# A gate projection ahead of the transposes, a norm in pieces, two merge blocks at the entry, and retention transposes on TensorE

## The chip, the cores and the metric

The kernel runs on one core of a Trainium2 chip. The metric is the device time of one execution in microseconds (us), taken over several runs; their median is compared.

## What is computed

Two transformer blocks follow each other on x of 1024 tokens by 1024 features, in float32. The first (neighbourhood attention beside a gated delta rule) is not touched by the change. The second reads, cut to what matters here:

```
h = rms_norm(x, norm_gain)
proj = einsum('bsd,dc->bsc', h, w_in)            # 1024 -> 10240 columns
(sb_q, sb_k, sb_v, sb_g, r_q, r_k, r_v, r_g, m_sb, m_ret) = split(proj)
qa, ka = rms_norm(heads(sb_q), q_gain), rms_norm(heads(sb_k), k_gain)      # 8 heads of 128
out_a = merge(stick_breaking_attention(qa, ka, heads(sb_v))) * silu(sb_g)
qb, kb = rotary(heads(r_q)), rotary(heads(r_k)) * RET_KEY_DIM ** -0.5      # 4 heads of 256
ret = chunkwise_retention(qb, kb, heads(r_v))
#   out   = (q * q_decay) @ state + (q k^T * intra_decay) @ v
#   state = state * chunk_decay + (k * k_decay)^T @ v
out_b = merge(rms_norm(ret, ret_out_gain)) * silu(r_g)
merged = sigmoid(m_sb + b0) * (out_a @ w_branch_sb) + sigmoid(m_ret + b1) * (out_b @ w_branch_ret)
x = x + merged @ w_out
```

## The kernel before, in words

Every large product runs in three passes: both operands are split into a high and a low part, and TensorE (PE) sums high·high, high·low and low·high in one PSUM bank. A product over 1024 features therefore takes 24 matmuls for each bank. The activations `h2T` (high `h2h`, low `h2l`) stand in SBUF with the features on the partitions. Weights are loaded in units of 128 rows and split either by ScalarE (ACT) and VectorE (DVE), lines 67 and 68, or by GpSimd (POOL), lines 70 and 71.

PSUM has three banks "a" for projections, two "z", and one each of "t", "o" and "p". Code is written in stages, and a scheduler then fixes the order of the instructions on each engine ahead of the run; at run time each engine works through its list in that order and waits where an input is late.

The stages after the first block, with their places in the profiled span:

- **Output projection and norm** (740 to 830 us). The tokens are worked on as two sets: set 0 is the two middle quarters, set 1 the outer two. Blocks of 128 output features are computed in set 0 and then, in the order 4 to 7 and 0 to 3, in set 1 (`out_blocks`, L859). Each is added to x on DVE (`residual`, L866), which frees its PSUM bank. `normalize` makes the RMS norm of one set: the squares' sum over features goes through PE (L897, L903), a reciprocal root goes through POOL (L125, L126), and then eight times DVE scales a block (L909), ACT takes its high part, and POOL or DVE its low part (L911).
- **Stick-breaking heads** (830 to 1340 us), eight in a row. A head projects q, k and v for eight groups of 128 tokens (`dense_tok`, L102), takes their norm (ACT L980, POOL L125 and L126, DVE L986), which frees the bank, and after every fourth group turns q and k by PE transposes (L993). Head 0 works by token set, so that it can begin with set 0 before set 1 is normed, and its gate projection stands in the same loop (L1003). The attention itself uses PE transposes into the banks "t" and "p" (L1050).
- **Merge projection** (`merge_logits`, L112 and L956): its quarter 0 follows the heads, the other three follow retention. Each quarter is four column blocks of 48 matmuls, 128 partitions by 512.
- **Retention** (1400 to 1940 us), four heads; `ret_proj` projects and rotates q and k (L1095 to L1100: DVE products, POOL sums, tile `ro`) and projects v (L102, L1109). `ret_chain` works in two groups of four chunks for each head. In each group k is turned so that tokens stand on partitions (`kf`), scaled and split into `kd` (ACT L1154, DVE L1155), and multiplied with v into the state (L1184, L1190, L1195). The chunk outputs `ot` (L1178) are turned back into `ob`, scaled (ACT L1201) and gated (POOL L1202). Both turns go through `dve_transpose`, 16 DVE instructions on 32x32 blocks (L132). `kf` and `ob` share one buffer.
- **Branches and output** (to 2279 us).

Of the kernel before, what the change touches and what calls it, by code (L numbers as in the profile page):

```python
# [11 lines left out]
F32 = mybir.dt.float32  # L12
# [7 lines left out]
P = 128  # L20
# [16 lines left out]
def tile_kernel(ctx: ExitStack, tc: tile.TileContext, I: dict, out: bass.AP, dbg=None, stop=None):  # L37
# [161 lines left out]
    sm = ctx.enter_context(tc.tile_pool(name="sm", bufs=1))  # L199
# [675 lines left out]
    sc_.__exit__(None, None, None)  # L875
    naB.__exit__(None, None, None)
# [6 lines left out]
    with tc.tile_pool(name="dd", bufs=1) as dd:  # L883
        XB = 10

        def square_sum(qa, xo, first):
            if first:
                nc.scalar.activation(out=qa, in_=xo, func=AF.Square)
                return
            sq = dd.tile([P, 512], F32, tag="sq", name="sq", bufs=2)  # L890
            nc.scalar.activation(out=sq, in_=xo, func=AF.Square)
            nc.vector.tensor_tensor(out=qa, in0=qa, in1=sq, op=ALU.add)

        def normalize(s, xs, qa):
            ps = bank("z")
            for j in range(4):
                nc.tensor.matmul(ps[:, 2 * j:2 * j + 2], lhsT=qa[:, j * P:(j + 1) * P], rhs=ones2, start=True, stop=True)  # L897
            rt_ = dd.tile([P, 4], F32, tag="rt", name="rt_", bufs=2)
            nc.vector.tensor_copy(out=rt_, in_=ps[:, 0:8:2])
            rsqrt_small(rt_, rt_, 1.0 / T, EPS, 4)  # L900
            pr = bank("t")
            for j in range(4):
                nc.tensor.matmul(pr[:, j * P:(j + 1) * P], lhsT=rt_[:, j:j + 1].to_broadcast([P, P]), rhs=ident,  # L903
                                 start=True, stop=True)
            rs = dd.tile([P, 512], F32, tag="rs", name="rs")
            nc.scalar.copy(out=rs, in_=pr)
            for k in range(NK):
                hi, lo = [token_set(h[:, k, :], s) for h in h2T]
                nc.vector.scalar_tensor_tensor(out=xs[k], in0=xs[k], scalar=gain2[:, k:k + 1], in1=rs, op0=ALU.mult, op1=ALU.mult)  # L909
                nc.scalar.copy(out=hi, in_=set2(xs[k]))  # L910
                (nc.gpsimd, nc.vector)[k % 2].tensor_tensor(out=lo, in0=set2(xs[k]), in1=f32(hi), op=ALU.subtract)  # L911

        xs = {}
        qa = dd.tile([P, 512], F32, tag="qa", name="qa")
        for b in range(4):
            xs[b] = dd.tile([P, 512], F32, tag="xo", name="x0", bufs=XB)
            nc.sync.dma_start(out=set2(xs[b]), in_=token_set(d_x1[b], 0))
            square_sum(qa, xs[b], b == 0)
        us = load_units(I["w_out"], 512, 512, fast=True)
        for b in range(4, 8):  # L920
            xs[b] = residual(dd, "xo", XB, out_blocks(us, 0, (b,))[0], 0, b)
            square_sum(qa, xs[b], False)
        normalize(0, xs, qa)
        xs = {}
        qa = dd.tile([P, 512], F32, tag="qa", name="qa")
        for half in (1, 0):
            if half == 0:
                us = load_units(I["w_out"], 0, 512, fast=True)
            for b in range(4 * half, 4 * half + 4):
                xs[b] = residual(dd, "xo", XB, out_blocks(us, 1, (b,))[0], 1, b)  # L930
                square_sum(qa, xs[b], b == 4)
        normalize(1, xs, qa)
# [14 lines left out]
    mp = ctx.enter_context(tc.tile_pool(name="mp", bufs=1))  # L947
    bm = mp.tile([P, 16], F32, name="bm")
    nc.sync.dma_start(out=bm, in_=I["b_merge_2"])

    def merge_logits(q):
# [11 lines left out]
    with tc.tile_pool(name="sb", bufs=1) as sb, tc.tile_pool(name="sr", bufs=1, side="right") as sr:  # L963
# [4 lines left out]
        for h in range(8):  # L968
# [4 lines left out]
            for n_, (m, acc) in enumerate(dense_tok(h2T, us, 0, 384, order=order)):  # L973
                j = n_ % 4
                if j == 0:
                    sq4 = sr.tile([P, 4, 256], F32, tag="sq", name="sq", bufs=2)
                sq = sq4[:, j, :]
                ss = sr.tile([P, 2], F32, tag="ss", name="ss", bufs=2)
                for a in range(2):
                    nc.scalar.activation(out=sq[:, a * P:(a + 1) * P], in_=acc[:, a * P:(a + 1) * P], func=AF.Square,  # L980
                                         accum_out=ss[:, a:a + 1])
                rsqrt_small(ss, ss, 1.0 / P, EPS, 2)
                nc.scalar.copy(out=v[0][:, m, :], in_=acc[:, 256:384])
                nc.vector.tensor_tensor(out=v[1][:, m, :], in0=acc[:, 256:384], in1=f32(v[0][:, m, :]), op=ALU.subtract)
                for a in range(2):
                    nc.vector.scalar_tensor_tensor(out=sq[:, a * P:(a + 1) * P], in0=acc[:, a * P:(a + 1) * P],  # L986
                                                   scalar=ss[:, a:a + 1], in1=gqk[:, a, :], op0=ALU.mult, op1=ALU.mult)
                if j == 3:
                    sl = slice((m - 3) * P, (m + 1) * P)
                    for a in range(2):  # L990
                        qa = bank("a")
                        for jj in range(4):
                            nc.tensor.transpose(qa[:, jj * P:(jj + 1) * P], sq4[:, jj, a * P:(a + 1) * P], ident)  # L993
                        hi, lo = [t_[:, sl] if h else token_set(t_, n_ // 4) for t_ in qk[a]]
                        if h == 0:
                            qa = set2(qa)
                        nc.scalar.copy(out=hi, in_=qa)
                        nc.vector.tensor_tensor(out=lo, in0=qa, in1=f32(hi), op=ALU.subtract)
                if j == 3 and h == 0:
                    acc = bank("a")  # L1000
                    for k in range(NK):
                        for i, (x, y) in enumerate(((0, 0), (1, 0), (0, 1))):
                            nc.tensor.matmul(acc, lhsT=us[k][:, y, 384:512], rhs=token_set(h2T[x][:, k, :], n_ // 4),  # L1003
                                             start=(k == 0 and i == 0), stop=(k == NK - 1 and i == 2))
                    gv = mp.tile([P, 512], F32, tag="lg", name="gv", bufs=2)
                    nc.scalar.copy(out=gv, in_=acc)
                    nc.sync.dma_start(out=token_set(d_ga[h], n_ // 4), in_=set2(gv))
# [57 lines left out]

    merge_logits(0)
# [4 lines left out]
    with tc.tile_pool(name="rt", bufs=1) as rt:  # L1071
# [61 lines left out]
        def ret_chain(h, tiles):  # L1133
            qTs, kTs, vs = tiles
            state = None
            for g in range(2):
# [14 lines left out]
                kf = rt.tile([P, 4, 256], F32, tag="ob", name="kf")  # L1151
                dve_transpose(kf.rearrange("p n (b c) -> p b n c", b=2), kT.rearrange("p b (n c) -> p b n c", n=4))
                kf, kh, kl = [t_.rearrange("p a b -> p (a b)") for t_ in [kf] + kd]
                nc.scalar.activation(out=kh, in_=kf, func=AF.Copy, scale=rdv[:, h, 0:1])  # L1154
                nc.vector.scalar_tensor_tensor(out=kl, in0=kf, scalar=rdv[:, h, 0:1], in1=f32(kh),  # L1155
                                               op0=ALU.mult, op1=ALU.subtract)
# [51 lines left out]
    for q in range(1, 4):  # L1208
        merge_logits(q)
# [130 lines left out]
```

## Time and profile before

| | us |
|---|---|
| median of 3 runs | 2288.43 |
| lowest and highest | 2281.9, 2291.71 |
| the profiled execution's own time | 2281.08 |
| its span | 2279.4 |

The page of the profile gives each engine's busy time as a share of the span. Its matmul durations overlap each other, since PE is pipelined: the time from the start of one to the start of the next is what a matmul costs, and the chain that ended last gives that in its piece for a row of matmuls.

### The profile page before, as it was taken

To read this page: it belongs to the slowest core of one execution; us is meant where nothing else is said; L and a number is where in the kernel's file an instruction comes from. 1 tells how busy PE (TensorE), PEld (TensorE's weight loads), DVE (VectorE), ACT (ScalarE), POOL (GpSimd) and SP (SyncE) were. 2 spreads that over 40 slices of the span, in tenths; PEclk is the share of its full clock that TensorE was granted. 3 is DMA by queue.
4 is the path that set the end of the run, shared out by engine and by line. 5 is a ranking of instruction groups with operands and counts; after the bars stand their busy time and mean duration, and the time that the engine had idled before them with its cause. 6 is when DMAs were issued, how large, how long until landed. Compare 5 with 4: busy or idle time off the path is not lost.

```text
span 2279.4 us, 33389 instructions
## 1 busy us (share of the span) xinstructions
PE 2171.1 (95%) x12197; PEld 1872.3 (82%) x12197; DVE 1222.5 (54%) x2228; ACT 763.6 (33%) x1904; POOL 1107.4 (49%) x1435
## 2 busy tenths in 40 slices
PE   7999888899999989999999999999989999999999
PEld 7777777687888878899999988888878788788887
DVE  4688789943457474556566541417474744321321
ACT  5344433445455233334344331112222222321200
POOL 6668787762003253333344442537575744444531
PEclk9999999999999999999999999999999999999999
DMA  4256830045386441111111113111333232654432
GB/s 131 85 155 163 206 109 26 36 118 165 103 301 228 148 131 47 54 33 36 56 56 52 56 61 103 37 65 56 130 112 129 84 107 93 222 171 153 148 107 102
DMA packets 238788, 249.23 MB, mean 109 GB/s; under 512 B 40032, under 2 KB 173856, under 8 KB 238368
## 3 DMA queue, kind: packets, MB, share of 16 engines
q1 hardware_dynamic: 238624, 247.10, 34.2%
q8 instruction: 96, 1.57, 0.3%
q14 instruction: 68, 0.56, 0.1%
HBM read 171.51 MB, written 75.53 MB: 108 GB/s over the span
## 4 chain that ended last, share of the span: by engine, by line
PE 54%; POOL 5%; issue 3%; DMA 2%; DVE 2%; ACT 1%; SPq 0%; POOLq 0%; ACTq 0%
PE acc L112 29%; PE acc L102 13%; PE acc L859 3%; PE po L1055 2%; PE pz L1023 2%; POOL wu L71 1%; POOL wu L70 1%; PE pt L1050 1%; PE pt L1171 1%; DMA d_oag<-oa 1%; DMA oa<-d_oa 1%; PE acc L1003 1%; POOL ob L1202 1%; PE pp L1050 0%; PE acc L120 0%
## 5 line engine op out<-in xcount | busy, mean ns | idle before, releaser
L112 PE MATMUL acc<-h2h,wu 128*128 128x512 f32 x1504 | 460.1, 396 | 0.7 <-POOL wu L71 0.4
L102 PE MATMUL acc<-wu,h2h 128*128 128x384 f32 (+1 forms) x1536 | 370.0, 324 | 6.8 <-DVE v L1109 4.0
L71 POOL TENSOR_TENSOR wu<-raw,wu 128x512 fp32r<-128x512 f32 (+3 forms) x268 | 364.1, 1367 | 7.0
L70 POOL TENSOR_SCALAR wu<-raw 128x512 fp32r<-128x512 f32 (+3 forms) x268 | 206.4, 773 | 330.1 <-PE acc L112 249.1
L112 PEld LDWEIGHTS acc<-h2h,wu 128*128 128x128 f32 x1504 | 282.1, 188 | 65.4 <-ACT lg L956 1.2
L102 PEld LDWEIGHTS acc<-wu,h2h 128*128 128x128 f32 x1536 | 268.0, 191 | 12.7 <-DVE v L1109 4.9
L112 PE MATMUL acc<-h2l,wu 128*128 128x512 f32 x752 | 278.3, 395 | 0.0
L102 PE MATMUL acc<-wu,h2l 128*128 128x384 f32 (+1 forms) x768 | 246.0, 321 | 0.0
L102 PE MATMUL acc<-wu,h1hi 128*128 128x384 f32 (+2 forms) x768 | 192.0, 333 | 12.6 <-DVE kS L518 6.7
L112 PE MATMUL acc<-h1hi,wu 128*128 128x512 f32 x512 | 165.8, 412 | 6.8 <-ACT pad L315 3.3
L125 POOL TENSOR_SCALAR ss<-ss 128x2 f32<-128x2 f32 (+2 forms) x136 | 37.1, 273 | 277.6 <-ACT sq L980 218.8
L112 PEld LDWEIGHTS acc<-h2l,wu 128*128 128x128 f32 x752 | 141.2, 188 | 31.1
L102 PEld LDWEIGHTS acc<-wu,h1hi 128*128 128x128 f32 x768 | 137.1, 195 | 17.0 <-issue 8.0
L102 PEld LDWEIGHTS acc<-wu,h2l 128*128 128x128 f32 x768 | 146.1, 190 | 1.9
L102 PE MATMUL acc<-wu,h1lo 128*128 128x384 f32 (+2 forms) x384 | 126.7, 333 | 0.0
L112 PEld LDWEIGHTS acc<-h1hi,wu 128*128 128x128 f32 x512 | 99.2, 195 | 31.7 <-ACT pad L315 4.4
L126 POOL TENSOR_TENSOR ss<-ss,mhalf 128x2 f32<-128x2 f32 (+2 forms) x136 | 119.2, 877 | 8.6
L112 PE MATMUL acc<-h1lo,wu 128*128 128x512 f32 x256 | 96.9, 407 | 0.0
L980 ACT ACTIVATE sq<-acc 128x128 f32<-128x128 f32 x128 | 35.6, 289 | 128.5 <-PE acc L102 124.4
L320 DVE SCALAR_TENSOR_TENSOR cv<-pad,c_conv_w,cv 128x1024 f32<-128x1024 f32 x48 | 76.6, 1596 | 1.1
L112 PE MATMUL acc<-oah,wu 128*128 128x512 f32 x256 | 76.9, 396 | 0.0
L1055 PE MATMUL po<-wT,v 128*128 128x512 f32 (+3 forms) x288 | 74.7, 351 | 1.7 <-DVE wT L1053 1.3
(546 smaller groups left out, 4471.5 us busy)
## 6 DMA issues: line engine op xcount, KB each, us to landing
raw<-in_w_in_dram SPq DMA_DIRECT2D x192, 256.0 KB, 2.9
d_pk<-sct SPq DMA_DIRECT2D x24, 512.0 KB, 4.3
raw<-in_w_out_dram SPq DMA_DIRECT2D x40, 256.0 KB, 2.6
wsa<-d_pk SPq DMA_DIRECT2D x16, 512.0 KB, 5.5
wsb<-d_pk SPq DMA_DIRECT2D x16, 512.0 KB, 7.6
d_sg<-lg SPq DMA_DIRECT2D x32, 256.0 KB, 2.5
sg<-d_sg SPq DMA_DIRECT2D x32, 256.0 KB, 3.6
raw<-in_w_in_dram SPq DMA_DIRECT2D x32, 192.0 KB, 2.7
```

The costliest lines, as they stand in the source:

```text
L70: nc.gpsimd.tensor_scalar(out=u[:, 0, :], in0=raw, scalar1=1.0, scalar2=0.0, op0=ALU.mult, op1=ALU.add)
L71: nc.gpsimd.tensor_tensor(out=u[:, 1, :], in0=raw, in1=f32(u[:, 0, :]), op=ALU.subtract)
L102: nc.tensor.matmul(acc[:, :n], lhsT=hT[a][:, k, m * P:(m + 1) * P], rhs=us[k][:, b, c0:c0 + n], start=(k == 0 and i == 0), stop=(k == NK - ...
L112: nc.tensor.matmul(accs[half], lhsT=us[k][:, b, c0:c0 + P], rhs=hT[a][:, k, half * 512:(half + 1) * 512], start=(k == 0 and i == 0), stop= ...
L125: nc.gpsimd.tensor_scalar(out=dst, in0=src, scalar1=mul, scalar2=eps, op0=ALU.mult, op1=ALU.add)
L126: nc.gpsimd.tensor_tensor(out=dst, in0=dst, in1=mhalf[:, :eshape], op=ALU.pow)
L320: nc.vector.scalar_tensor_tensor(out=cv, in0=pad[:, i:i + T], scalar=conv_w[:, blk, i:i + 1], in1=cv, op0=ALU.mult, op1=ALU.add)
L859: nc.tensor.matmul(acc, lhsT=us[k][:, y, (b % 4) * P:(b % 4 + 1) * P], rhs=token_set(mT[x][:, k, 0:T], s), start=(k == 0 and i == 0), stop ...
L980: nc.scalar.activation(out=sq[:, a * P:(a + 1) * P], in_=acc[:, a * P:(a + 1) * P], func=AF.Square, accum_out=ss[:, a:a + 1])
L1003: nc.tensor.matmul(acc, lhsT=us[k][:, y, 384:512], rhs=token_set(h2T[x][:, k, :], n_ // 4), start=(k == 0 and i == 0), stop=(k == NK - 1 a ...
L1023: nc.tensor.matmul(pz[:, :w], lhsT=qk[0][a][:, i * P:(i + 1) * P], rhs=qk[1][b][:, c0:c0 + w], start=(x == 0), stop=(x == 2))
L1055: nc.tensor.matmul(po[:, i0 * P:512], lhsT=v[a][:, c0 // P + kb, :], rhs=wT[b][:, :n], start=(diag and kb == 0 and x == 0), stop=(diag == ...
```

## The change

It has four parts.

1. `normalize` becomes a generator, and pieces of it are asked for after each block of the output projection (set 0) and after each token group of head 0 (set 1). Some pools open and close at other places, and the number of `xo` buffers goes from 10 to 9.
2. In head 0 the gate projection is written ahead of the transposes of q and k.
3. Two of the sixteen merge blocks (12 and 13) are computed at the entry, by token set, from weights of their own in a pool "fp": 16 more split instructions on POOL and 8 DMAs of 128 KB. Three of their four banks are asked for in head 0 and the last at head 1. The last quarter of the merge projection after retention keeps two blocks.
4. In retention both turns go to PE, as 16 transposes of 128x128 for each group, into bank "p". ACT and DVE read them from PSUM. `dve_transpose` is gone, and `kf` too.

```diff
-    def dve_transpose(dst, src):
-
-        for a in range(4):
-            for b in range(4):
-                nc.vector.transpose(out=dst[32 * b:32 * b + 32, :, :, 32 * a:32 * a + 32],
-                                    in_=src[32 * a:32 * a + 32, :, :, 32 * b:32 * b + 32])
...
+        nc.scalar.copy(out=rs, in_=pr)
+        yield 1
+        for k in range(NK):
...
+            (nc.gpsimd, nc.vector)[k % 2].tensor_tensor(out=lo, in0=set2(xs[k]), in1=f32(hi), op=ALU.subtract)
+            yield 1
...
+    norm = normalize(0, xs, qa)
...
+            square_sum(qa, xs[b], b == 4)
+            take(norm, 3 if b == 4 else 1)
+    drain(norm)
+    norm = normalize(1, xs, qa)
...
+    def early_logits():
+
+        us = load_units(I["w_in_2"], 8192 + 12 * P, 256, pool=fp, tag="fu")
+        for s in range(2):
+            for b in range(2):
+                acc = bank("a")
+                for k in range(NK):
+                    for i, (x, y) in enumerate(((0, 0), (1, 0), (0, 1))):
+                        nc.tensor.matmul(acc, lhsT=us[k][:, y, b * P:(b + 1) * P], rhs=token_set(h2T[x][:, k, :], s),
+                                         start=(k == 0 and i == 0), stop=(k == NK - 1 and i == 2))
...
+                yield 1
+
+    early = early_logits()
...
+                if h == 0:
+                    take(norm, 3)
...
+                if j == 3 and h == 0:
+                    acc = bank("a")
...
+                    nc.sync.dma_start(out=token_set(d_ga[h], n_ // 4), in_=set2(gv))
+                    if n_ == 3:
+                        drain(norm)
+                        dd_.__exit__(None, None, None)
+                        sb = sbs.enter_context(tc.tile_pool(name="sb", bufs=1))
+                    take(early, 1 + (n_ == 3))
                 if j == 3:
                     sl = slice((m - 3) * P, (m + 1) * P)
                     for a in range(2):
...
-                if j == 3 and h == 0:
-                    acc = bank("a")
...
+            if h == 1:
+                drain(early)
...
-                kf = rt.tile([P, 4, 256], F32, tag="ob", name="kf")
-                dve_transpose(kf.rearrange("p n (b c) -> p b n c", b=2), kT.rearrange("p b (n c) -> p b n c", n=4))
...
+                for x in range(2):
+                    pk = bank("p")
+                    for j in range(2):
+                        for b in range(2):
+                            n = 2 * x + j
+                            nc.tensor.transpose(pk[:, j * 256 + b * P:j * 256 + (b + 1) * P], kT[:, b, n * P:(n + 1) * P], ident)
...
+                    nc.scalar.activation(out=kh, in_=pk, func=AF.Copy, scale=rdv[:, h, 0:1])
...
-                dve_transpose(ob, ot.rearrange("p n (b c) -> p b n c", b=2))
...
+                    pt = bank("p")
+                    for j in range(4):
+                        nc.tensor.transpose(pt[:, j * P:(j + 1) * P], ot[:, j, b * P:(b + 1) * P], ident)
...
-        merge_logits(q)
+        merge_logits(q, range(2, 4) if q == 3 else range(4))
```

`take(g, n)` runs n steps of a generator, and `drain(g)` the rest. The order of the compiled instructions changes at three places.

**The set 0 norm on DVE**, behind the second block of set 1 (about 790 us in the span). Before, the sum of x and the second block, and one sum of squares, stand ahead of the eight scalings L909:

```order
L899 COPY rt__7971<-pz 128x4
L866 TENSOR_TENSOR xo<-acc,xo 128x512
L892 TENSOR_TENSOR qa<-qa,sq 128x512
L909 SCALAR_TENSOR_TENSOR x_7780<-x_7780,c_norm_gain_7774,rs 128x512
...
L909 SCALAR_TENSOR_TENSOR xo<-xo,c_norm_gain_7774,rs 128x512 x4
...
L911 TENSOR_TENSOR h2l<-x_7793,h2h 128x512
L866 TENSOR_TENSOR xo<-acc,xo 128x512
L911 TENSOR_TENSOR h2l<-xo,h2h 128x512
```

In the changed kernel (L866 is now L860, L909 is L911, L911 is L913):

```order
L900 COPY rt__8011<-pz 128x4
L911 SCALAR_TENSOR_TENSOR x_7789<-x_7789,c_norm_gain_7775,rs 128x512
...
L911 SCALAR_TENSOR_TENSOR xo<-xo,c_norm_gain_7775,rs 128x512 x4
...
L913 TENSOR_TENSOR h2l<-x_7802,h2h 128x512
L860 TENSOR_TENSOR xo<-acc,xo 128x512
L913 TENSOR_TENSOR h2l<-xo,h2h 128x512
L68 TENSOR_TENSOR wu<-raw,wu 128x512
L860 TENSOR_TENSOR xo<-acc,xo 128x512
```

The sum of the second block, which frees its bank, has moved behind all eight scalings and two low parts.

**Head 0 on PE**, where its first four token groups end. Before, the eight transposes of q and k stand directly behind the last projection, and the gate projection behind them:

```order
L102 MATMUL acc<-wu,h2h 128x384 x2
L102 MATMUL acc<-wu,h2l 128x384
L993 MATMUL acc<-ident,sq 128x128 x8
L1003 MATMUL acc<-h2h,wu 128x512
L1003 MATMUL acc<-h2l,wu 128x512
```

In the changed kernel 24 matmuls of the gate (L1013) and 48 of the merge blocks (L969) come first, and the norm's broadcast for set 1 (L904) stands ahead of the last projections:

```order
L904 MATMUL pt<-ident,rt__8423 128x128 x4
...
L102 MATMUL acc<-wu,h2h 128x384 x2
L102 MATMUL acc<-wu,h2l 128x384
L1013 MATMUL acc<-h2h,wu 128x512
...
L969 MATMUL acc<-h2h,wu 128x512
L969 MATMUL acc<-h2l,wu 128x512
...
L1028 MATMUL acc<-ident,sq 128x128 x8
```

On POOL the reciprocal roots of head 0 (`ss`) and of the set 1 norm (`rt`) stand there; before, nothing else was among them:

```order
L125 TENSOR_SCALAR rt__8306<-rt__8306 128x4
L126 TENSOR_TENSOR rt__8306<-rt__8306,mhalf 128x4
L125 TENSOR_SCALAR ss<-ss 128x2
L126 TENSOR_TENSOR ss<-ss,mhalf 128x2
L125 TENSOR_SCALAR ss<-ss 128x2
```

and now the splits of the early merge weights (128x256) do:

```order
L70 TENSOR_SCALAR wu<-raw 128x256 x2
L71 TENSOR_TENSOR wu<-raw,wu 128x256 x2
L125 TENSOR_SCALAR ss<-ss 128x2
L70 TENSOR_SCALAR wu<-raw 128x256
L125 TENSOR_SCALAR ss<-ss 128x2
L125 TENSOR_SCALAR rt__8423<-rt__8423 128x4
L126 TENSOR_TENSOR ss<-ss,mhalf 128x2
L71 TENSOR_TENSOR wu<-raw,wu 128x256
L126 TENSOR_TENSOR ss<-ss,mhalf 128x2
L70 TENSOR_SCALAR wu<-raw 128x256
L126 TENSOR_TENSOR rt__8423<-rt__8423,mhalf 128x4
```

The `rt` root has moved behind the roots of two token groups, with splits between them.

**Retention**, at the change from one head to the next. On DVE before, the two turns (16 instructions each) stand among the rotation (L1095 to L1098) and ahead of the state's updates:

```order
L1178 TENSOR_SCALAR ot<-pt,rdv,ss 128x256
L1098 TENSOR_TENSOR ro<-ro,cosT 128x512
L132 STREAM_TRANSPOSE ob<-ot 32x8x32 x16
L1095 TENSOR_TENSOR rtmp<-ro,cosT 128x512
...
L1095 TENSOR_TENSOR rtmp<-ro,cosT 128x512
L132 STREAM_TRANSPOSE kf<-ro 32x2x4x32 x16
L1178 TENSOR_SCALAR ot<-pt,rdv,ss 128x256
L1097 TENSOR_TENSOR rtmp<-ro,sinT 128x512
L1155 SCALAR_TENSOR_TENSOR kd<-kf,rdv,kd 128x1024
```

On PE in the changed kernel, in the first group of head 0, the transposes of k (L1185) fill bank "p" twice, with 15 matmuls of the v projection between the two fills:

```order
L1172 MATMUL pz<-ro 128x128
L1185 MATMUL pp<-ident,ro 128x128
L1172 MATMUL pz<-ro 128x128 x7
L1185 MATMUL pp<-ident,ro 128x128 x3
L102 MATMUL acc<-wu,h2h 128x256
...
L102 MATMUL acc<-wu,h2l 128x256
L1185 MATMUL pp<-ident,ro 128x128 x4
L1196 MATMUL pt<-v,wT 128x256
```

The turns have left DVE's list, and each fill of bank "p" has to be read by ACT and DVE before PE may start the next.

## Rows read from the trace of the kernel before

**Rows 1.** The page: engines' busy us; one group (busy us, mean ns, idle before).

```profile
PE 2171.1 (95%) x12197; PEld 1872.3 (82%) x12197; DVE 1222.5 (54%) x2228; ACT 763.6 (33%) x1904; POOL 1107.4 (49%) x1435
...
L71 POOL TENSOR_TENSOR wu<-raw,wu 128x512 fp32r<-128x512 f32 (+3 forms) x268 | 364.1, 1367 | 7.0
```

**Rows 2.** Stages: window, length, busy us (PE, PEld, DVE, ACT, POOL), clock, DMA.

```profile
800.00:860.00 60.00, 51.14 (x244) 43.62 (x243) 39.06 (x54) 19.59 (x48) 31.60 (x32) 0.94 0.38 119
...
1430.00:1980.00 550.00, 525.41 (x2845) 449.16 (x2844) 287.98 (x466) 132.22 (x275) 313.09 (x313) 0.98 0.31 103
```

**Rows 3.** PE's waits, 740 to 1000 us: total us, times, longest.

```profile
PE acc L993 <- DVE sq L986: 7.8, 5, 4.9
PE acc L859 <- DVE xo L866: 1.8, 1, 1.8
...
PE acc L859 <- ACT wu L67: 0.9, 1, 0.9
```

**Rows 4.** DVE's timeline, 797 to 807 us: start, us, instruction, count, idle before.

```profile
797.13 6.20 DVE L909 SCALAR_TENSOR_TENSOR xo<-xo,c_norm_gain,rs 128x512 f32<-128x512 f32 x4
803.25 2.78 DVE L911 TENSOR_TENSOR h2l<-x,h2h 128x512 fp32r<-128x512 f32 x2
805.96 0.68 DVE L866 TENSOR_TENSOR xo<-acc,xo 128x512 f32<-128x512 f32 x1
```

**Rows 5.** Entry of head 0, windows of 4 us; columns as in rows 2.

```profile
844.00:848.00 4.00, 2.83 (x17) 2.56 (x15) 4.00 (x4) 2.29 (x4) 3.83 (x5) 1.00 0.00 0
848.00:852.00 4.00, 0.25 (x1) 0.18 (x1) 4.00 (x6) 1.92 (x7) 3.83 (x4) 0.83 0.00 0
852.00:856.00 4.00, 2.82 (x9) 1.95 (x9) 3.07 (x8) 1.07 (x2) 0.37 (x2) 0.50 0.04 6
856.00:860.00 4.00, 4.00 (x16) 3.13 (x16) 0.71 (x2) 0.00 (x0) 0.00 (x0) 0.82 0.00 0
```

**Rows 6.** The chain that ended last, in order of time: start, us, what.

```profile
855.02 6.74 PE acc L1003 x24
861.76 16.34 PE acc L102 x93
...
881.43 0.73 PE acc L993 x2
882.16 6.83 PE acc L1003 x24
...
920.69 0.45 PE pt L1050 x4
...
946.27 5.57 PE acc L112 x24
```

**Rows 7.** Groups by line, 1150 to 2279 us: busy us, mean ns, idle before.

```profile
L132 DVE STREAM_TRANSPOSE kf<-ro 32x256 f32<-32x256 f32 x128 | 55.8, 436 | 24.5 <-DMA d_ob<-ob 22.8
...
L1050 PE MATMUL pt<-ident,B 128*128 128x128 f32 x77 | 14.8, 275 | 0.0
...
L1154 ACT ACTIVATE kd<-kf,rdv 128x1024 fp32r<-128x1024 f32 x8 | 9.2, 1151 | 44.4 <-DVE kf L132 44.4
```

**Rows 8.** PE's waits, 1425 to 1985 us; columns as in rows 3.

```profile
PE acc L102 <- DVE v L1109: 4.0, 4, 1.7
PE pt L1163 <- DVE ot L1178: 4.0, 3, 2.0
PE pz L1143 <- POOL ro L1100: 3.2, 4, 1.2
PE po L1184 <- ACT kd L1154: 3.1, 2, 2.1
...
PE po L1184 <- DVE kd L1155: 2.3, 3, 1.0
```

**Rows 9.** Two windows of retention; columns as in rows 2.

```profile
1464.00:1474.00 10.00, 7.15 (x31) 6.37 (x31) 9.69 (x21) 2.38 (x5) 5.20 (x5) 0.55 0.26 80
...
1684.00:1694.00 10.00, 6.71 (x52) 5.92 (x51) 8.82 (x9) 1.25 (x2) 10.00 (x8) 1.00 0.33 107
```

More of the change, by code (lines that the diff above doesn't have):

```diff
@@ L197, in tile_kernel @@
     d_x1 = dram.tile([NK, P, T], F32, name="d_x1")
-    sm = ctx.enter_context(tc.tile_pool(name="sm", bufs=1))
+    sm_ = tc.tile_pool(name="sm", bufs=1)
+    sm = sm_.__enter__()
     hp = tc.tile_pool(name="hp", bufs=1, side="right")
@@ L882, in tile_kernel @@
     gain2 = load_const("norm_gain_2", [P, NK])
[L883 to L932, printed above, removed]
@@ new lines, in tile_kernel, with square_sum @@
+    mp = ctx.enter_context(tc.tile_pool(name="mp", bufs=1))
+    bm = mp.tile([P, 16], F32, name="bm")
+    nc.sync.dma_start(out=bm, in_=I["b_merge_2"])
+    fp_ = tc.tile_pool(name="fp", bufs=8)
+    fp = fp_.__enter__()
+    dd_ = tc.tile_pool(name="dd", bufs=1)
+    dd = dd_.__enter__()
+    XB = 9
+    def square_sum(qa, xo, first):
+        if first:
+            nc.scalar.activation(out=qa, in_=xo, func=AF.Square)
+            return
+        sq = dd.tile([P, 512], F32, tag="sq", name="sq", bufs=2)
+        nc.scalar.activation(out=sq, in_=xo, func=AF.Square)
+        nc.vector.tensor_tensor(out=qa, in0=qa, in1=sq, op=ALU.add)
@@ new lines, in normalize @@
+    def normalize(s, xs, qa):
+        ps = bank("z")
+        for j in range(4):
+            nc.tensor.matmul(ps[:, 2 * j:2 * j + 2], lhsT=qa[:, j * P:(j + 1) * P], rhs=ones2, start=True, stop=True)
+        rt_ = dd.tile([P, 4], F32, tag="rt", name="rt_", bufs=2)
+        nc.vector.tensor_copy(out=rt_, in_=ps[:, 0:8:2])
+        rsqrt_small(rt_, rt_, 1.0 / T, EPS, 4)
+        pr = bank("t")
+        for j in range(4):
+            nc.tensor.matmul(pr[:, j * P:(j + 1) * P], lhsT=rt_[:, j:j + 1].to_broadcast([P, P]), rhs=ident,
+                             start=True, stop=True)
+        rs = dd.tile([P, 512], F32, tag="rs", name="rs")
+        nc.scalar.copy(out=rs, in_=pr)
+        yield 1
+        for k in range(NK):
+            hi, lo = [token_set(h[:, k, :], s) for h in h2T]
+            nc.vector.scalar_tensor_tensor(out=xs[k], in0=xs[k], scalar=gain2[:, k:k + 1], in1=rs, op0=ALU.mult, op1=ALU.mult)
+            nc.scalar.copy(out=hi, in_=set2(xs[k]))
+            (nc.gpsimd, nc.vector)[k % 2].tensor_tensor(out=lo, in0=set2(xs[k]), in1=f32(hi), op=ALU.subtract)
+            yield 1
@@ new lines, in tile_kernel @@
+    xs = {}
+    qa = dd.tile([P, 512], F32, tag="qa", name="qa")
+    for b in range(4):
+        xs[b] = dd.tile([P, 512], F32, tag="xo", name="x0", bufs=XB)
+        nc.sync.dma_start(out=set2(xs[b]), in_=token_set(d_x1[b], 0))
+        square_sum(qa, xs[b], b == 0)
+    us = load_units(I["w_out"], 512, 512, fast=True)
+    for b in range(4, 8):
+        xs[b] = residual(dd, "xo", XB, out_blocks(us, 0, (b,))[0], 0, b)
+        square_sum(qa, xs[b], False)
+    norm = normalize(0, xs, qa)
+    xs = {}
@@ L933, in tile_kernel @@
+    qa = dd.tile([P, 512], F32, tag="qa", name="qa")
+    for half in (1, 0):
+        if half == 0:
+            us = load_units(I["w_out"], 0, 512, fast=True)
+        for b in range(4 * half, 4 * half + 4):
+            xs[b] = residual(dd, "xo", XB, out_blocks(us, 1, (b,))[0], 1, b)
+            square_sum(qa, xs[b], b == 4)
+            take(norm, 3 if b == 4 else 1)
+    drain(norm)
+    norm = normalize(1, xs, qa)
     hp.__exit__(None, None, None)
@@ L946, in tile_kernel, with merge_logits @@
     d_sg = dram.tile([16, P, T], F32, name="d_sg")
[L947 to L951, printed above, removed]
+    def merge_logits(q, bs=range(4)):
         us = load_units(I["w_in_2"], 8192 + 512 * q, 512)
-        for b in range(4):
+        for b in bs:
             for half, acc in enumerate(dense_col(h2T, us, b * P)):
@@ L962, in tile_kernel @@
     last_sb = None
-    with tc.tile_pool(name="sb", bufs=1) as sb, tc.tile_pool(name="sr", bufs=1, side="right") as sr:
+    with tc.tile_pool(name="sr", bufs=1, side="right") as sr, ExitStack() as sbs:
         gqk = sr.tile([P, 2, P], F32, name="gqk")
@@ L998, in tile_kernel @@
                         nc.vector.tensor_tensor(out=lo, in0=qa, in1=f32(hi), op=ALU.subtract)
-                if j == 3 and h == 0:
-                    acc = bank("a")
[L1001 to L1007, printed above, removed]
+            if h == 1:
+                drain(early)
             for half, acc in enumerate(dense_col(h2T, us, 384) if h else ()):
@@ L1064, in tile_kernel @@
         return
+    fp_.__exit__(None, None, None)
     merge_logits(0)
```

20 lines of the change are left out of this document (15 added, 5 removed).

## The prediction

> **What bounds the kernel now.** I read the engines' busy shares first. PE is busy 95% of the span, DVE 54% and POOL 49% [rows 1], so only PE's lost time and PE's own work can move the end. The stages show where PE loses time. From 800 to 860 us it is busy 51.14 of 60 us at a granted clock of 0.94, and in retention, 1430 to 1980 us, 525.41 of 550 us at 0.98 [rows 2]. These are the two places that the change touches. The waits name the causes at the first: 7.8 us for DVE's scaled q and k (L986) ahead of the transposes L993, and 1.8 us for a residual sum (L866) and 0.9 us for a weight split in the projection before it [rows 3]. In retention the listed waits are spread over many lines, with DVE behind four of the five largest, or ACT behind DVE, and POOL's rotation behind one [rows 8].
>
> All terms below are made against the profiled execution, 2281.08 us, which stands 7.35 us under the median of 2288.43 us. The sum is carried over to the median at the end.
>
> **Set 0 norm.** In the changed order the second block's residual sum stands behind the eight scalings and two low parts. In the profile that work ends at 805.96 us, where the next residual sum now stands [rows 4], so the sum will end near 806.6 us. PE has three banks "a"; the fifth block needs the second one's bank. Four blocks of 24 matmuls at 5.57 us each (the price of such a row [rows 6]) end near 802 us. PE then waits about 4.6 us where it now loses 1.8 and 0.9 us [rows 3], both of which the longer wait covers. Term: **+1.9 us**, bounds 0 and +3.
>
> **First stall at the entry.** Between 844 and 860 us PE is busy 2.83 + 0.25 + 2.82 + 4.00 = 9.90 of 16 us, so 6.1 us are idle; DVE is at work 4.00 of 4 us in the first two of these windows, and this is the set 1 norm, ahead of the L986 that the transposes need [rows 5]. After the window in which PE did 0.25 us of work, the granted clock is 0.50, the lower level (1.2 GHz), and the gate's 24 matmuls take 6.74 us where 24 of the same shape take 5.57 at the higher level [rows 5, 6]: 1.2 us more. The change puts these 24 (5.6 us) and 48 merge matmuls (48 x 0.232 = 11.1 us) between the last projection and the transposes. 16.7 us of work cover a lateness of 6.1 us, so both losses go: **-7.3 us**.
>
> What is late next is the norm of set 1. Its root now stands on POOL among the splits of the early weights, and its broadcast on PE behind more projections. A unit of 512 columns costs 1.37 us in L71 and less in L70 [rows 1], so eight units of half the width cost at most about 11 us of POOL, and several of them stand ahead of the first root. If the scalings begin 8 us later, the second merge block can reach a bank whose L986 is queued behind them on DVE. Nothing in the trace shows this order, so I bound it: 0 if the 11.2 us of gate and first merge block cover it, and 8 us if the whole shift shows. I take the side nearer to cover: **+2 us**. The 8 DMAs more of 128 KB stand in a stretch in which the DMA share is 0.00 to 0.04 [rows 5], and cost nothing unless the first unit comes late; then POOL's list stops, and the same +8 holds.
>
> **Second stall.** The same turn for set 1 ends at 861.76 + 16.34 = 878.10 us, and the last two transposes start at 881.43; six others (0.65 us) run in between. So 2.7 us are lost, and the gate behind it takes 6.83 instead of 5.57 us [rows 6]. The gate and one merge block (24 + 24 matmuls, 11 us) now stand in between: **-3.9 us**, bounds -2.7 and -4.5.
>
> **The merge blocks** are moved: 96 matmuls of 0.232 us, 22.3 us, are added at the entry and leave the end. Their net is 0, since PE is full in both places.
>
> **128 transposes on PE.** Four in a row take 0.45 us in the chain [rows 6], or 0.11 us each, and these are float32 of the same shape: 128 x 0.11 = **+14.1 us**. They are pure addition, since PE did none of this before.
>
> The group's row gives a mean duration of 275 ns [rows 7], which would make 35.2 us; but durations overlap on PE, and the chain's steps do not. The Trainium skill, "TensorE: Matmul & The Clock Gate", on transposes, gives about 275 ns for one in a kernel's context and says that they do not engage the full clock. By it the sum would be 21 us higher. This trace agrees with the number as a duration and not as a price: the four in the chain take 0.45 us.
>
> **What retention gets back.** PE is idle 24.6 us there, and a clock of 0.98 over 550 us is another 11 us [rows 2]; 36 us are lost. One place shows the mechanism: from 1464 to 1474 us DVE is busy 9.69 us, PE runs 31 matmuls in 7.15 us, and the granted clock is 0.55 [rows 9]; one turn of 16 at 436 ns [rows 7] is 7.0 us of DVE. DVE spends 55.8 us on `kf`, and as many instructions of the same kind on `ob`: 111.6 us in all. ACT waits 44.4 us for `kf` ahead of `kd` and DVE itself 22.8 us for the buffer that `kf` shares with `ob` [rows 7]. Both go. Of the five largest waits DVE holds 4.0 + 4.0 + 2.3 and, through ACT's `kd`, 3.1, so 13.4 of 16.6 us; POOL holds 3.2 [rows 8]. With the smaller ones I put the share that goes at 0.7 of the 36 us, or 25 us. POOL is what remains: near the change of heads it is busy 10.00 of 10 us [rows 9], and the waits for its rotation and splits stay.
>
> The new wait is bank "p". It has one buffer, filled four times in each of eight groups, and ACT and DVE must read a fill before the next. Reading half of `kd` should take about half of ACT's 1.15 us [rows 7] and a similar time on DVE. Most second fills have over ten merge or projection matmuls ahead of them on PE, 2.3 us at 0.232 us each. I take 3 us over all groups. Term: **-22 us**; bounds -9.4 (only the waits for v, 4.0, and for `kd`, 3.1 + 2.3, go [rows 8]) and -33 (all but POOL's).
>
> **The sum:** 1.9 - 7.3 + 2 - 3.9 + 14.1 - 22 = -15.2 us, 2265.9 us on the basis of the profiled execution and **2273 us** in medians.
>
> **Rivals.**
>
> - *The transposes eat the gain* (0.23). DVE was late together with POOL, whose 10.00 of 10 us [rows 9] does not shrink, so removing DVE's share uncovers POOL. Then only the -9.4 us go, and the sum is 1.9 - 7.3 + 2 - 3.9 + 14.1 - 9.4 = -2.6, or 2286 us: no change. For it speaks that no listed wait is longer than 2.1 us, so that DVE and POOL end close together [rows 8]; against it, that in the window of 1464 us, where the clock is low, POOL is busy only 5.20 us [rows 9].
> - *Bank "p" becomes the wait* (0.12): slower. PE stands in order; the reader of a fill on DVE can be queued behind rotation products. If in each of the 16 turns the second fill waits w, the sum is -15.2 - 3 + 16w. It is slower by more than 0.5% (11.4 us, about what a measurement can tell from no change) from w = 1.9 us; at 2.5 us the time is 2310 us. Against it speaks the work that stands between the fills.
> - *A transpose costs its mean duration* (0.05): 21 us more, 2294 us, no change by that bound.
> - *Everything goes* (0.08): -33 in retention and no wait at the entry, which makes -28 us or 2260 us.
>
> My forecast has 0.52. Its own range is 2263 to 2281 us: the entry's +2 can be 0 or 8, and retention -26 to -17. The range that is to hold 8 in 10 reaches up over the no-change cases, to 2292, and down to 2254, below "everything goes"; outside are the slower rival, most of the dear transposes, and what is faster still. Faster by over 0.5% means under 2277 us: 0.8 of the forecast, all of "everything goes", and a part of the first rival's spread, 0.55 together. Slower, over 2299.9 us, is 0.13: the bank and a few dear transposes. The rest, 0.32, is the same.
>
> **What the new profile would show.** Right: no wait of 4.9 us ahead of the transposes in head 0, and no window at 0.50 near 852 us; a wait of 4 to 5 us for a residual sum near 802 us; DVE some 110 us less busy in retention, PE's idle time there under 12 us, and four transposes in about 0.45 us; the last merge stage 22 us shorter. Wrong: waits of PE for ACT's or DVE's reads of bank "p" that sum to over 10 us; waits for POOL (`ro`, `wu`, `ss`) that grow by what DVE's lose; or a stall ahead of the early merge blocks for `wu` or for the norm of set 1.

## The result, and the profile after

The changed kernel takes 2254.41 us (median of 4 runs, 2252.17 to 2256.41) against 2286.27 us before: ratio 0.9863, 95% interval 0.9846 to 0.988, or 1.4% faster, some 31 us. I had forecast 15 us. Run once more (e12) it gave 0.9842 (0.982 to 0.9864). The page of the first profiled execution (the one used below where no run is named):

```profile
span 2250.5 us, 33410 instructions
PE 2163.0 (96%) x12325; PEld 1882.8 (84%) x12325; DVE 1102.5 (49%) x1980; ACT 766.0 (34%) x1912; POOL 1105.4 (49%) x1451
```

PE runs 128 matmuls more than in [rows 1] and is still busy 8.1 us less. That is the first hint: 128 transposes at 0.11 us should have added 14 us. The two stages of [rows 2], the entry in a window moved by the 9 us that it starts later:

```profile
809.00:869.00 60.00, 55.17 (x259) 47.98 (x260) 31.74 (x49) 18.05 (x46) 37.26 (x45) 0.94 0.46 141
1430.00:1980.00 550.00, 540.86 (x3057) 472.57 (x3056) 175.16 (x224) 136.92 (x287) 313.57 (x325) 1.00 0.34 107
```

In retention DVE is 112.8 us less busy, PE idles 9.1 us in place of 24.6, and its clock is 1.00 in place of 0.98. PE's waits, at the entry and in retention:

```profile
PE acc L853 <- DVE xo L860: 4.4, 1, 4.4
PE acc L102 <- ACT lg L972: 2.2, 1, 2.2
PE acc L102 <- DVE sq L1007: 1.6, 1, 1.6
```

```profile
PE po L1217 <- DVE st L1223: 2.8, 2, 2.2
PE pt L1204 <- ACT ss__17476 L1227: 1.7, 1, 1.7
PE acc L102 <- DVE v L1138: 1.5, 3, 0.8
PE acc L102 <- POOL wu L71: 1.4, 1, 1.4
PE po L1217 <- ACT kd L1187: 0.7, 1, 0.7
```

The 7.8 us ahead of the transposes [rows 3] are gone; the wait for the residual sum is there (4.4 us; I had said 4.6). In retention POOL's rotation, which I had said would stay [rows 8], is no longer in the list at all.

The clock of the entry's window is 0.94 as before. The low clock at 852 us [rows 5] is gone, and from 837 to 889 us every window of 4 us shows 1.00; but a new low stretch stands at the wait for the residual sum (columns as in rows 2):

```profile
808.00:812.00 4.00, 0.00 (x0) 0.00 (x0) 4.00 (x4) 0.62 (x1) 4.00 (x4) 0.81 0.37 118
812.00:816.00 4.00, 3.73 (x9) 2.99 (x10) 4.00 (x7) 1.26 (x2) 0.75 (x1) 0.50 0.58 189
816.00:820.00 4.00, 4.00 (x17) 3.21 (x16) 2.19 (x4) 1.15 (x2) 0.59 (x1) 0.84 0.89 293
```

The second hint stands in code that the change does not touch. The last long piece of the chain, almost all of it branches and output, before and then in the changed kernel:

```profile
1978.96 285.49 PE acc L112 x1224
```

```profile
2000.04 235.71 PE acc L112 x1032
```

Per matmul that is 0.2332 and 0.2284 us. I call this time from one start to the next the step. Both stretches run the same lines on the same engine, with almost nothing to wait for and the granted clock at 1.00, the higher level (2.4 GHz); before and then in the changed kernel:

```profile
1979.00:2264.00 285.00, 285.00 (x1223) 230.05 (x1224) 55.01 (x68) 40.36 (x60) 114.48 (x111) 1.00 0.42 141
```

```profile
2000.00:2236.00 236.00, 235.96 (x1034) 194.44 (x1035) 45.63 (x62) 30.03 (x47) 93.70 (x93) 1.00 0.41 137
```

From head 0 on, the 128x512 matmuls of L112 take 4 to 5 ns less; in the first block and the output projection their step has not changed.

Where the time went, by the starts of PE's instructions in the profiled executions (us):

| | before | changed | e1 | e4 | e7 | e8 | e9 |
|---|---|---|---|---|---|---|---|
| to head 0's first projection | 827.8 | 837.0 | 830.4 | 828.0 | 833.8 | 840.0 | 830.8 |
| heads, to their last matmul | 566.7 | 575.2 | 563.0 | 567.2 | 556.4 | 552.8 | 552.5 |
| quarter 0 and retention | 543.2 | 531.4 | 539.8 | 536.8 | 540.6 | 530.0 | 531.9 |
| to the end | 341.7 | 306.9 | 336.4 | 333.7 | 342.5 | 326.8 | 327.4 |

The first row holds the first block, whose unchanged code ends with the delta rule's last PE instruction at 751 to 760 us in these executions, so what follows that is compared below. One profiled execution stands behind each column; the medians hold the first block's scatter too.

### The profile page after: what moved, and what is told of

Same layout as the page of the kernel before. It is cut to its first block, busy times and chain, and to the rows that moved or that the text cites. A ratio compares the mean times of both kernels' runs of the same rounds, so it can differ in the third digit from the quotient of the medians.

```text
span 2250.5 us, 33410 instructions
## 1 busy us (share of the span) xinstructions
PE 2163.0 (96%) x12325; PEld 1882.8 (84%) x12325; DVE 1102.5 (49%) x1980; ACT 766.0 (34%) x1912; POOL 1105.4 (49%) x1451
## 4 chain that ended last, share of the span: by engine, by line
PE 68%; DVE 11%; POOL 6%; issue 5%; DMA 5%; ACT 2%; SPq 1%; POOLq 0%; DVEq 0%; ACTq 0%
PE acc L112 29%; PE acc L102 17%; PE acc L853 3%; PE po L1083 2%; PE pz L1051 2%; DVE X L459 2%; DVE svt L457 2%; POOL wu L71 2%; DVE cv L314 1%; POOL wu L70 1%; DMA raw<-in_w_in_dram 1%; PE pz L546 1%; PE pt L563 1%; POOL ss L126 1%; PE pp L577 1%
## 5 line engine op out<-in xcount | busy, mean ns | idle before, releaser
L112 PE MATMUL acc<-h2h,wu 128*128 128x512 f32 x1440 | 438.4, 393 | 0.7 <-ACT lg L958 0.7
L112 PEld LDWEIGHTS acc<-h2h,wu 128*128 128x128 f32 x1440 | 269.5, 188 | 54.9 <-ACT lg L958 1.1
L112 PE MATMUL acc<-h2l,wu 128*128 128x512 f32 x720 | 265.2, 392 | 0.0
L112 PE MATMUL acc<-h1hi,wu 128*128 128x512 f32 x512 | 167.3, 416 | 6.8 <-ACT pad L309 3.2
L112 PEld LDWEIGHTS acc<-h2l,wu 128*128 128x128 f32 x720 | 135.0, 188 | 26.5
L112 PEld LDWEIGHTS acc<-h1hi,wu 128*128 128x128 f32 x512 | 100.4, 198 | 31.8 <-ACT pad L309 4.2
L112 PE MATMUL acc<-h1lo,wu 128*128 128x512 f32 x256 | 97.9, 411 | 0.0
L112 PE MATMUL acc<-oah,wu 128*128 128x512 f32 x256 | 76.1, 393 | 1.0 <-DVE sg L1275 0.6
L102 PEld LDWEIGHTS acc<-wu,h1lo 128*128 128x128 f32 x384 | 74.8, 195 | 0.4 <-issue 0.2
```

The lines of the kernel that those rows point to most:

```text
L102: nc.tensor.matmul(acc[:, :n], lhsT=hT[a][:, k, m * P:(m + 1) * P], rhs=us[k][:, b, c0:c0 + n], start=(k == 0 and i == 0), stop=(k == NK - ...
L112: nc.tensor.matmul(accs[half], lhsT=us[k][:, b, c0:c0 + P], rhs=hT[a][:, k, half * 512:(half + 1) * 512], start=(k == 0 and i == 0), stop= ...
```

## The experiments

**Theories.** A: the pool `sm` is now closed ahead of `h2T`, which puts `h2T` and all later buffers of that side 1664 bytes lower, and these addresses set the step of the wide matmuls. B: the faster step comes from less work on DVE, or from the one execution.

**e1: the layout alone.**

```diff
# the kernel before
-    sm = ctx.enter_context(tc.tile_pool(name="sm", bufs=1))
+    sm_ = tc.tile_pool(name="sm", bufs=1); sm = sm_.__enter__()
...
-    sc_.__exit__(None, None, None)
+    sc_.__exit__(None, None, None); sm_.__exit__(None, None, None)
```

> The kernel before with one edit: the pool sm is closed ahead of the pool of h2T, as in the changed kernel, so that h2T and all later buffers of that side lie 1664 bytes lower; the order of the instructions stays. Theory A (the addresses set the step of the wide matmuls): the step of the 128x512 matmuls behind 840 us falls from 0.2325 to about 0.228 us as in the changed kernel; about 3,300 of them x 4.5 ns and 1,536 of 128x384 x 1.7 ns give -17 us, so about 2268. Theory B (the pace came from the other parts, through less work on DVE, or from the one execution): the step stays at 0.2325 and the time at 2286.

2272.14 us, ratio 0.9937 (0.992 to 0.9953). The long piece of its chain:

```profile
2019.20 235.70 PE acc L112 x1032
```

0.2284 us per matmul: A holds. An edit that reorders nothing and removes nothing is worth 0.6%. It is less than the 17 us expected: in retention PE's idle time rises from 24.2 to 29.0 us, so a part of what the faster steps give is lost there to waits.

**e2 and e5: other addresses in the changed kernel.**

```diff
-    hp2 = ctx.enter_context(tc.tile_pool(name="hp2", bufs=1))
+    hp2 = ctx.enter_context(tc.tile_pool(name="hp2", bufs=1)); hp2.tile([P, 256], F32, name="shift")   # e5: [P, 32]
```

> The changed kernel with 1024 unused bytes ahead of h2T, so that h2T and later buffers lie 1024 bytes higher (640 bytes lower than before the change); nothing else. Theory A: the step of the 128x512 matmuls changes from 0.228, toward 0.2325 us if the low step belongs to the distance of 40960 bytes between h2T and the weights, and the time rises by up to 17 us to about 2271. Theory B: no change, 2254.

> The changed kernel with 128 unused bytes ahead of h2T. The run with 1024 bytes kept the low step, so what matters must repeat within 1024 bytes. Seen from the weights' units, h2T lies at a whole multiple of 512 bytes in the changed kernel and 128 bytes beside one before. If this offset decides, 128 bytes bring the step of the 128x512 matmuls on h2T back to 0.2325 us and cost some 12 to 17 us, 2267. If the cause is the old place itself and not the offset, the step stays at 0.228 and the time at 2251.

e2: 2247.07 us, ratio 0.9824 (0.9807 to 0.9842); the step stays low, against what I expected of A. e5: 2263.91 us, ratio 0.9916 (0.9889 to 0.9943); the step is back at 0.2332. Their chains, e2 first:

```profile
1986.57 240.32 PE acc L112 x1051
```

```profile
1985.28 263.09 PE acc L112 x1128
```

So the address itself does not decide; what does must be the same after 1024 bytes and differ after 128.

**e6: the step as a function of the start.**

```diff
+    def probe(o, s):
+        acc = bank("a")
+        nc.tensor.matmul(acc[:, :64], lhsT=wt[:, 0, 0:P], rhs=mv[:, 0:64], start=True, stop=True)
+        for i in range(16):
+            nc.tensor.matmul(acc, lhsT=wt[:, i % 2, s:s + P], rhs=mv[:, o:o + 512], start=(i == 0), stop=(i == 15))
+    for s in (0, 32):
+        for o in range(32):
+            probe(8 * o, s)
+    for s in range(16):
+        probe(0, 8 * s)
```

> The changed kernel with a row of 80 groups of 16 matmuls behind its end, whose results nobody reads: 128x512 on a fixed tile, its start moved in steps of 32 bytes over 1 KB, with the weights at two places, and then the weights' start moved over 512 bytes. The step of each group is read. If the offset between the two operands decides, the pattern over the moved start shifts with the weights' place; if the moving operand's own address decides, it does not; if neither, all groups step alike. About 300 us longer.

2555.91 us (one run). PE's timeline at the starts 128, 160, 192 and 224 bytes, with the weights at 0:

```profile
2262.35 3.99 PE L1309 MATMUL acc<-mgh,wu 128*128 128x512 f32 x16
2266.18 0.19 PE L1307 MATMUL acc<-mgh,wu 128*128 128x64 f32 x1
2266.21 3.97 PE L1309 MATMUL acc<-mgh,wu 128*128 128x512 f32 x16
2270.01 0.19 PE L1307 MATMUL acc<-mgh,wu 128*128 128x64 f32 x1
2270.05 3.88 PE L1309 MATMUL acc<-mgh,wu 128*128 128x512 f32 x16
2273.77 0.19 PE L1307 MATMUL acc<-mgh,wu 128*128 128x64 f32 x1
2273.80 3.98 PE L1309 MATMUL acc<-mgh,wu 128*128 128x512 f32 x16
```

and at 32, 64 and 96 bytes with the weights 128 bytes further:

```profile
2373.34 3.98 PE L1309 MATMUL acc<-mgh,wu 128*128 128x512 f32 x16
...
2377.19 3.89 PE L1309 MATMUL acc<-mgh,wu 128*128 128x512 f32 x16
...
2380.95 3.98 PE L1309 MATMUL acc<-mgh,wu 128*128 128x512 f32 x16
```

One group is 0.1 us (6 ns for each matmul) shorter than its neighbours, and when the weights move by 128 bytes, the short one moves from 192 to 64. `mgh` starts 64 bytes beside a multiple of 256 from the weights, so both short groups are those where the distance between the two operands is a multiple of 256 bytes. Over all 80 groups, without the first step of each, the mean steps are 227.4 to 229.6 ns there, 228.9 to 230.1 ns where the data lie 64 bytes further, and 232.4 to 234.3 ns at the six other offsets; the pattern repeats every 256 bytes. In the built programs `h2h` lies 128 bytes beside a multiple of 256 from the weights before and in e5, and at a multiple in the changed kernel, e1 and e2; `oah` moved from 192 to 64. The distance decides.

The Trainium skill, "TensorE: Matmul & The Clock Gate", section "Step-by-step: what each phase is for", says that PE reads weights and moving data through two independent ports, so that loading the next weights takes no read bandwidth from the running matmul. By that, the place of the weights should not matter. In the scan it does: with every operand resident, the other engines idle and the granted clock at 1.00, the step depends on where the weights lie relative to the data. That the two reads meet in the memory behind the ports is argued, not shown.

**e3 and e4: the turns.** e3 is the changed kernel with `dve_transpose`, `kf` and the reads of `ob` as before; e4 the kernel before with both turns on PE as in the change, and nothing else.

```diff
# e4, on the kernel before (e3 is the reverse on the changed kernel)
-                dve_transpose(kf.rearrange("p n (b c) -> p b n c", b=2), kT.rearrange("p b (n c) -> p b n c", n=4))
+                            nc.tensor.transpose(pk[:, j * 256 + b * P:j * 256 + (b + 1) * P], kT[:, b, n * P:(n + 1) * P], ident)
...
-                dve_transpose(ob, ot.rearrange("p n (b c) -> p b n c", b=2))
+                        nc.tensor.transpose(pt[:, j * P:(j + 1) * P], ot[:, j, b * P:(b + 1) * P], ident)
```

> The changed kernel with the retention turns put back on DVE (no transposes on PE there). My forecast's terms (+14.1 for the transposes, -22 for retention) say +8 us, 2262. Theory A agrees, since the traces leave about -11 us for this part beside the pace. A rival that gives the transposes all of the unforecast gain says +25 us, 2279.

> The kernel before with the retention turns on PE and nothing else changed. Theory A: -8 to -11 us, 2276, with the step of the 128x512 matmuls still at 0.2325 us. Theory B, that fewer DVE instructions quicken PE's steps: the step falls to 0.228 in retention and the time to about 2262.

e3: 2266.09 us, ratio 0.9906 (0.9888 to 0.9923). e4: 2268.26 us, ratio 0.9917 (0.9902 to 0.9932), with the step of before in its chain:

```profile
1965.42 285.39 PE acc L112 x1224
```

DVE does less work in e4, and the step is the old one, so B falls. The turns give more than I had said. By the table retention and what follows are 14.4 us shorter in e4 than before, and 18.7 us shorter in the changed kernel than in e3 (857.0 us); with e12's execution in its place that is 16.3 us. The ratios, which hold the first block's scatter, give 19 us for e4, and for e3 10 to 15 us against the two of the changed kernel. I go by the stages, 14 to 19 us. PE's waits in e4:

```profile
PE po L1181 <- DVE st L1187: 1.7, 2, 1.1
PE acc L102 <- POOL wu L71: 1.4, 1, 1.4
PE acc L102 <- DVE v L1102: 1.0, 2, 0.7
PE pz L1136 <- POOL ro L1092: 0.9, 1, 0.9
PE pz L1136 <- POOL ro L1093: 0.7, 1, 0.7
```

**e11: which part of DVE's lateness.**

```diff
# the kernel before
-                kf = rt.tile([P, 4, 256], F32, tag="ob", name="kf")
+                kf = rt.tile([P, 4, 256], F32, tag="kf", name="kf")
```

> The kernel before with kf in a buffer of its own, so that DVE's turn of k no longer waits for ob's write to memory; turns stay on DVE. If the 22.8 us of DVE's wait for that buffer are what made retention late, this gains much of what e4 gained, -10 to -19 us. If DVE's own time for the turns (111.6 us) is the cause, it gains 0 to -3 us.

2310.03 us, ratio 1.011 (1.0091 to 1.013): slower, which neither side had said. DVE's turn of k now waits 1.8 us in place of 24.5, and PE waits longer:

```profile
L132 DVE STREAM_TRANSPOSE kf<-ro 32x256 f32<-32x256 f32 x128 | 55.7, 435 | 1.8
```

```profile
PE acc L102 <- DVE v L1109: 16.7, 7, 5.8
PE acc L102 <- POOL wu L71: 8.7, 6, 2.6
PE pz L1143 <- POOL ro L1099: 6.1, 3, 3.6
PE pz L1143 <- POOL ro L1100: 4.2, 5, 1.6
```

With its own buffer the scheduler puts the turns earlier on DVE, ahead of some of the v copies that free PE's banks and of some of the rotation's products. So the edit changed two things, the wait and the order, and neither was measured alone. What it shows is that taking away 22.7 us of DVE's waiting need not gain anything. That the loss comes from turns of 7 us ahead of short work that PE and POOL wait for fits the rows, but is argued.

**e7: the gate alone.** In the kernel before, the gate's block of lines stands ahead of the transposes, as in the change; nothing else.

```diff
+                if j == 3 and h == 0:
+                    acc = bank("a")
...
                 if j == 3:
                     sl = slice((m - 3) * P, (m + 1) * P)
```

> The kernel before with the gate projection of head 0 ahead of the transposes, and nothing else. 24 matmuls (5.6 us) cover most of the first stall of 6.1 us and the second of 2.7 us, and the half clock behind both goes: -8 to -10 us, about 2277 to 2279, the step at 0.2325 us. A rival, that the norm of set 1 is what the entry waits for in any order, gives 0.

2274.02 us, ratio 0.9952 (0.9933 to 0.9972), or 11 us; the heads are 10.3 us shorter. That is what I expected, or slightly more. PE's waits around its entry:

```profile
PE acc L859 <- DVE xo L866: 1.8, 1, 1.8
PE acc L1002 <- DVE sq L986: 1.6, 2, 1.1
```

**e8 and e9: the early merge blocks and the order of the set 0 norm.**

```diff
# e8, on the changed kernel
-    early = early_logits()
+    early = iter(())
...
-        merge_logits(q, range(2, 4) if q == 3 else range(4))
+        merge_logits(q)
# e9: e8 and
-    XB = 9
+    XB = 10
```

> The changed kernel with all sixteen merge blocks after the heads and retention again. My forecast puts the cover of the two stalls on the gate's 5.6 us and the blocks' 11 us together; without the blocks 0.5 us of the first stall is uncovered and POOL has 11 us less of splits, so the time is 2251 plus or minus 2. If the blocks carry the entry, it is 6 to 10 us longer.

> The changed kernel without the early merge blocks (as e8) and with ten xo buffers, so that the residual sum of set 1's second block stands ahead of the eight scalings again. My forecast's term for that order is +1.9 us, so this is 2 us (up to 3) faster than e8, some 2242 to 2248. If the wait of 4.4 us only moves to the next block, it is e8's time.

e8: 2244.14 us, ratio 0.983 (0.9806 to 0.9854). e9: 2242.25 us, ratio 0.9813 (0.979 to 0.9836), beside 2248.47 us for the changed kernel on the same chip. e8 is faster than I expected either way: the blocks do not help. e8's heads (552.8 us) are as long as those of the changed kernel less the 22.3 us of the blocks (552.9). Without the blocks PE still waits 2.8 us ahead of the transposes; with them it waits 2.2 us for a bank that a merge block holds (L972). Up to 1000 us its waits behind the one for the residual sum add up to 3.4 us in e8 and 3.8 us in the changed kernel. So the gate alone gave the cover. And the blocks' absence at the end is worth 18.5 us, not 22.3 (the rest after the heads is 838.3 against 856.8 us). e8's chain runs through the end without a break:

```profile
1955.45 279.42 PE acc L112 x1224
```

The changed kernel's leaves PE there, and goes through weights and `ob` from memory:

```profile
1980.76 3.05 DMA raw<-in_w_branch_sb_dram
...
1989.45 5.33 DMA oa<-d_ob
1994.80 1.06 ACT obh L1257
```

PE itself waits only 1.7 us there, against 0.4 in e8, so these waits explain 1.3 of the 3.8 us; the rest was not found, and is of the size by which two executions of the same code differ (856.8 us in e8, 859.3 in e9).

In e9 the wait for the residual sum is 1.9 us in place of 4.4, and from the delta rule's last PE instruction to head 0 the stage takes 77.0 us, as before (76.7), against 80.4 in the changed kernel and 79.6 in e8. The medians of e9 and e8 differ by the 2 us that I expected. By e9's order it is the ninth against the tenth buffer of `xo`, and not the norm in pieces, that put the residual sum behind the scalings.

**e10: the first block aligned too.**

```diff
# e9 and
-    ident = const.tile([P, P], F32, name="ident")
+    ident = const.tile([P, P], F32, name="ident"); const.tile([P, 32], F32, name="shift")
```

> e9 with 128 unused bytes ahead of the weights' units, so that in the first block too the activations lie at a multiple of 256 bytes from the weights. By the scan the step of its 1,344 matmuls of 128x512 falls from 0.2325 to 0.228 us or less, and of 768 of 128x384 by 1.7 ns: 6 to 8 us faster than e9. If the offset only matters behind 840 us for a reason of another kind, the time is e9's.

2241.29 us, ratio 0.9802 (0.9777 to 0.9827): e9's time. The step did fall. PE's timeline, e9 and then e10; each row shown is the third matmul behind the one above it:

```profile
70.42 0.39 PE L112 MATMUL acc<-h1lo,wu 128*128 128x512 f32 x1
...
71.12 0.40 PE L112 MATMUL acc<-h1lo,wu 128*128 128x512 f32 x1
...
71.83 0.39 PE L112 MATMUL acc<-h1lo,wu 128*128 128x512 f32 x1
```

```profile
70.32 0.39 PE L112 MATMUL acc<-h1lo,wu 128*128 128x512 f32 x1
...
71.00 0.39 PE L112 MATMUL acc<-h1lo,wu 128*128 128x512 f32 x1
...
71.68 0.39 PE L112 MATMUL acc<-h1lo,wu 128*128 128x512 f32 x1
```

0.705 against 0.68 us for three. But up to 751 us PE is busy 690.43 us in e9 and 685.57 in e10, and the delta rule's last PE instruction came at 753.8 and 756.0 us: the 5 us became idle time, since PE is not what ends the first block.

**e12: the changed kernel again.**

> The changed kernel once more, beside e9 and e10 on one chip. Its ratio of 0.9863 to the kernel before gives 2252 to 2256.

2248.47 us, 2245.05 to 2253.78, between 3 and 4 us under the range that I expected.

## Why the prediction was wrong, by its steps

- **The step that failed: the price of a matmul taken as fixed.** The prediction has 0.232 us for a matmul of the kernel before and of the changed one. A pool that closes earlier moved the operands to another distance, and the step fell to 0.228. No term stands for that. Alone (e1) it is worth 14 us by the ratio, 12 us by the stages of the profiled execution. Part 1 of the change names the pools that open and close elsewhere; I had read that as bookkeeping and priced it at nothing without naming what could make it matter. Without this term 17 to 22 us of gain are left, against my 15.
- **Retention, -22 us: mis-sized.** With transposes at 0.11 us (14.1 us; 8 in a row take 0.87 us in the changed kernel's chain), e4's 14.4 us mean that 28.5 us came back, and the difference to e3 means 32.8 (30.4 with e12): near my upper bound (-33). The sentence that "the waits for its rotation and splits stay" failed. Before, POOL's sum of the rotation (L1099) waits 14.4 us for DVE's products, so a part of POOL's lateness was DVE's, passed on; in e11, where DVE's turns stand earlier, PE waits longer for POOL, in e4 less long. Bank "p" as a wait does not appear, so the 3 us for it were not needed.

```profile
L1099 POOL TENSOR_TENSOR ro<-rtmp 128x512 f32<-128x512 f32 x16 | 25.8, 1611 | 14.5 <-DVE rtmp L1096 13.5 <-DVE rtmp L1097 0.9
```

- **The entry, -7.3 + 2 - 3.9 = -9.2 us: right in size.** e7 gives 10.3 us with the gate alone, and the low clock there is gone. That the cover needed the merge blocks was wrong.
- **The merge blocks, 0: wrong by about 4 us** by the profiled stages of e8. A third of that is waits of PE at the end, where fewer matmuls stand ahead of the branches; the rest stays open.
- **Set 0 norm, +1.9 us: mis-sized.** The wait is 4.4 us as forecast, and the 0.9 us for the weights are covered by it, as forecast. But the stage is 3.7 us longer. What I left out is the clock behind the wait: 11 matmuls from 812.27 to 817.13 us take 4.86 us, where 0.2325 us each makes 2.6, so 2.3 us more. I had priced the low clock at head 0's stall and not at the stall that I forecast myself.

```profile
812.27 0.80 PE L853 MATMUL acc<-mahi,wu 128*128 128x512 f32 x1 [4.38 <-DVE xo L860]
812.86 0.63 PE L853 MATMUL acc<-malo,wu 128*128 128x512 f32 x1
...
817.13 0.48 PE L853 MATMUL acc<-mahi,wu 128*128 128x512 f32 x1
```

- **A transpose's price: right**, and the mean duration (here 272 ns) was no price.
- **The ranges.** The forecast's own range, 2263 to 2281 us, does not follow from the bounds given for it: an entry of 0 or 8 and retention from -26 to -17 make 2267 to 2284. The measured 2254.41 us lies just inside the wide range's lower end, 2254, which stood below "everything goes". That it does is luck: the largest single part of what was missing is a term that the range did not have.

Together on the profiled basis, without the first block: layout -12, entry -10, retention -14 to -19, set 0 norm +4, blocks +4, which is -28 to -33. After the delta rule's last PE instruction the changed kernel is 34 us shorter (the span is 28.9 us shorter, and that instruction came 5.5 us later), in e12 32 us. The parts were measured singly, and their sum agrees with the whole only within the few us by which two executions of the same code differ.

## What to carry to other kernels

Before costing a change instruction by instruction, compare where its buffers lie: when pools open or close elsewhere, the distance of weights and moving data can change the step of the wide matmuls in stages that the diff does not touch. A pad (128 bytes in e5 and e10) is a cheap trial, but only stages in which PE sets the end give the gain back (e10). A wait for an engine that itself waits for another is not that engine's own: before leaving it in the sum, ask what the releaser was waiting for. And a stall that a change adds is priced like one that it removes: with the clock behind it.

## What was new of the hardware

With float32 operands of 128x512, PE's step at a granted clock of 1.00 was 227.4 to 229.6 ns when moving data and weights lay a multiple of 256 bytes apart, and 232.4 to 234.3 ns at most other distances (e6); in two kernels the same lines at that clock thus differed by 2%. And in e11 an added buffer that removed 22.7 us of waiting on DVE, and with it changed DVE's order, made the kernel 1.1% slower.
